# Halving the first gated-FFN weight unit, re-timing the weight and activation transfers, and adding the last outputs in DRAM

## The chip, the cores and the metric

The kernel is one launch on all eight cores of one Trainium2 chip (trn2). Each core works on its own prompt sequence and on 16 of the 128 sample tokens, with the same weights and without talking to the other cores. The metric is the device time of the slowest core, in microseconds (us). Executions of a program on all eight cores have a second, slower state here: the cores of one die run at a lower granted TensorE clock, and the time is some per cent longer.

The trace tells five engines apart: PE (TensorE, matrix products; "PEld" are its weight loads), DVE (VectorE), ACT (ScalarE), POOL (GpSimd) and SP (SyncE). The last two issue most of the DMAs.

## The reference, cut to what matters

```python
def _layer(x, buf_a, buf_b, h0, p):
    x = x + 0.5 * _rmsnorm(_swiglu(_rmsnorm(x, p['g_ffn1_pre']), ...), p['g_ffn1_post'])
    m, nba, nbb, hl = _mixer(_rmsnorm(x, p['g_mix_pre']), buf_a, buf_b, h0, p)
    x = x + _rmsnorm(m, p['g_mix_post'])
    x = x + 0.5 * _rmsnorm(_swiglu(_rmsnorm(x, p['g_ffn2_pre']), ...), p['g_ffn2_post'])
    return x, nba, nbb, hl

def _swiglu(x, w_gate, w_up, w_down):
    return (jax.nn.silu(x @ w_gate) * (x @ w_up)) @ w_down
```

The model width is 1024 (eight chunks of 128), the FFN width 2816 (22 "hidden blocks" of 128). A sequence has 2048 tokens and 16 meta tokens in front. Two places matter for this change: the first product, whose weights are the `gate` and `up` columns of hidden block 0, and the last line, a residual `x` plus a normed FFN output, which is what is stored.

## The kernel before

A core's 2080 tokens are cut into five streams of 414 to 418 tokens, which share three sets of activation buffers. The weights don't fit on the core, so they stream through a ring of ten slots, one "unit" of up to 128 x 2048 bf16 values per slot. The streams go through the layer in four groups. Group 0 (streams 0 and 1) reads the weights in fp32, casts them in the DMA and writes the bf16 form back to a scratch tensor `wsc`; later groups read the scratch. Stream 2 joins group 0 for the first `JOIN` units, so that the first hidden blocks have three streams to feed.

All instruction orders are fixed when the program is built: a list scheduler in the kernel's Python walks a model of the engines and of the DMA queues and picks what each engine issues next, steered by priority tables (`LAGS`, `STARTS`, `ENDS`, `CLASSES`). On the chip each engine then runs its list in that order and waits by semaphores.

```python
SIZES = [418, 418, 416, 414, 414]
GROUPS = [[0, 1], [2], [3], [4]]
BUFSET = [0, 1, 2, 0, 1]          # streams 3 and 4 take over the buffers of 0 and 1
NW = 10                           # slots of the weight ring
JOIN = 8
WARM = (44, 12, 10, 10, 40, 50)   # filler matmuls that keep TensorE busy at the start
X2_AFTER = 1
CAST_BW = 265e3; COPY_BW = 400e3  # bytes per us, the scheduler's model of the DMA

def issue_unit(g, u):
    n, off = UNIT_LIST[u][2], UNIT_OFF[u]
    v = V(wpool, lambda sl: wring[:, sl, :])                 # one slot of the ring
    src = wall if g == 0 else wsc
    S.dma("pool", lambda e: e.dma_start(out=v[0:n](), in_=src[:, off:off + n]), ..., cast=(g == 0))
    if g == 0:                                               # write the bf16 form back
        S.dma("sp", lambda e: e.dma_start(out=wsc[:, off:off + n], in_=v[0:n]()), [v], [("wsc", u)], n * 128 * 2)
    return v

def final_norm(st, acc):
    s, n, o, m = st.s, st.n, st.o, st.m
    rv = rms_finish(acc, m)
    step = 2 if st.last else 4
    events = []
    for oc in range(KC):
        yv = O32[s][:, oc * m:(oc + 1) * m]
        tv = newf()
        tt(tv[0:m], y32[s][:, oc, 0:m], rv[0:m], ALU.mult, m, ...)        # normed FFN output
        tt(yv, xs_view(st, oc, o, n), tv[0:m], ALU.add, m, ...)           # plus the residual
        if (oc + 1) % step == 0:
            ...                                                           # y store, issued by SP

def gu(st, hc, w, o):             # one hidden block of one stream
    ...
    ns = 8 if st.i == 0 and o == 0 and hc < 2 else 4 if hc < 2 else 1
    pG, pU, sg = newp(), newp(), newf()
    mm_split(pG[0:m], m, [wv(w, k * 128, 128) for k in range(KC)], rhs, rd, w, pG, ns)
    early = st.i == 0 and o == 0 and hc == 0
    mm_split(pU[0:m], m, [wv(w, (KC + k) * 128, 128) for k in range(KC)], rhs, rd, w, pU, ns, ...)
    if early:
        keep_warm(WARM[5], ["early"])       # 50 filler matmuls after stream 0's first block
    ...

# order of the first loads
first(-999.0, load_x, STREAMS[0], "sp", [])
head = [first(-998.0, issue_unit, 0, 0)]
first(-997.0, load_x, STREAMS[1], "pool", [R_xs(STREAMS[0], 3)])
head += [first(-997.0 + u, issue_unit, 0, u) for u in range(1, HEAD)]
```

## Time and profile before

The time was 1573.11 us (median of three runs, 1571.3 to 1598.96; the longest is in the slow state). From the first page of the profile of the slowest core: the span, the busy time of each engine with its share and its number of instructions, and the shares of the chain of waits that ended last.

```profile
span 1573.1 us, 27150 instructions; the slowest of 8 cores (1564.6 to 1573.1 us)
...
PE 1534.5 (98%) x8771; PEld 846.8 (54%) x8771; DVE 812.2 (52%) x1535; ACT 787.3 (50%) x1379; POOL 245.3 (16%) x465
...
PE 89%; DMA 5%; DVE 3%; issue 1%; ACT 1%; POOL 0%; DVEq 0%; SPq 0%; ACTq 0%; POOLq 0%
```

TensorE is the bound. Its 8,560 useful matmuls start 176 ns apart in the steady stretches (175.6 in the mean), which makes 1,503 us, so only about 70 us can be won by any change that leaves the matmuls alone. Most of them lie in four places.

| Where | What the trace shows | Lost there |
|---|---|---|
| head | few useful matmuls before 27.2 us | about 24 us (27.2 us less 16 x 0.176) |
| about 870 us | one gap, then half clock on six of the eight cores | 4 to 10 us, by core (time from the 4700th to the 4800th useful matmul, less 17.6) |
| tail | from the last matmul's start to the end | 14.5 us |
| small gaps elsewhere | | about 11 us |

The head, in the timeline view of TensorE (core 2). The columns are start, length, engine, source line, operation with its tiles, number of matmuls, and in brackets the idle time before and what ended it. "hy,wring" is useful work (activations with a weight slot), "qp,ones" are sums of squares for a norm, "ones" alone are fillers.

```profile
16.45 3.96 PE L652 MATMUL P<-hy,wring 128*128 128x418 bf16 x12 [2.06 <-DVE hy L684]
...
21.96 2.95 PE L652 MATMUL P<-ones 128*128 128x128 bf16 x50
...
27.21 54.13 PE L652 MATMUL P<-hy,wring 128*128 128x418 bf16 x304 [1.13 <-DMA wring<-wall]
82.16 0.34 PE L652 MATMUL P<-qp,ones 128*128 128x416 bf16 x1 [0.81 <-DVE qp L670]
```

The first hidden block of stream 0 starts at 16.45 us. Its last four matmuls stand between sums of squares of stream 1, which wait for that stream's input, fillers follow, and the second block starts at 27.21 us, when a weight unit from `wall` has landed. From there TensorE runs 54 us without a break, until stream 2 joins at 82 us with almost no wait.

The stall in the middle: TensorE's timeline on the same core, then that of SP, which issues the input of stream 3 (`xs<-xin`) and the outputs of stream 0 (`yout<-big`), 830 KB each.

```profile
867.15 2.97 PE L652 MATMUL P<-hy,wring 128*128 128x416 bf16 x16 [0.20 <-DMA wring<-wsc]
876.16 7.80 PE L652 MATMUL P<-hy,wring 128*128 128x416 bf16 x32 [6.04 <-DMA wring<-wsc]
```

```profile
854.30 0.33 SPq L740 DMA_DIRECT2D xs<-xin  x1
854.73 0.38 SPq L810 DMA_DIRECT2D yout<-big  x1
858.98 0.33 SPq L740 DMA_DIRECT2D xs<-xin  x1
859.40 0.41 SPq L810 DMA_DIRECT2D yout<-big  x1
```

TensorE stands for 6.04 us until a weight unit from the scratch lands. The 32 matmuls after that take 7.80 us where 5.6 would do: in the records of the clock it is at half there. The Trainium skill, "TensorE: Matmul & The Clock Gate", Part 1, says of the gate that answers to idleness that it knows only full and half, that the clock falls to half after about 3.4 us of idleness and needs about as long to come back. The half-clock stretches here are 3 to 10 us long. They show no fixed border in the length of a gap: in the run after, all eight cores have a gap of 2.21 or 2.22 us near 1230 us, shorter than the page's 3.4 us, and two of them show half clock behind it; in the run before, core 3 has none behind a gap of 3.89 us at 872 us. So a gap can cost more than its own length, but by how much differs from core to core.

The tail: VectorE's timeline (core 2), and from the view of DMAs in the last 20 us the line of the four y stores of the last stream (issuing queue, number, KB each, median us from issue to landing).

```profile
1560.30 0.59 DVE L670 TENSOR_TENSOR fp<-hy,fp 128x414 f32<-128x414 f32 x1 [4.09 <-ACT fp L666]
1561.00 0.59 DVE L670 TENSOR_TENSOR big<-xs,fp 128x414 f32<-128x414 f32 x1
...
1569.37 0.59 DVE L670 TENSOR_TENSOR big<-xs,fp 128x414 f32<-128x414 f32 x1
```

```profile
yout<-big SPq DMA_DIRECT2D x4, 414.0 KB, 2.4
```

The last matmul starts at 1558.6 us. After the norm's scale is known, VectorE makes 16 passes of 0.59 us, a product and a sum for each of the eight chunks, and each pair of chunks is stored when it is ready. VectorE sets the pace; only the last store is exposed.

### The profile page before, as it was taken

The page shows a single profiled execution, that of the slowest core. Times are in us where ns is not written, and L with a number is a line of the kernel's source. Part 1 is how long each engine was busy: PE and PEld are TensorE (multiplying, and loading weights), DVE is VectorE, ACT ScalarE, POOL GpSimd, SP SyncE. Part 2 cuts the span into 40 slices and gives each one's busy share as a digit, 9 for nine tenths or more (in the row PEclk, how much of TensorE's full clock was granted, in tenths as well). Part 3 has the DMA queues.
Part 4 walks back from the last instruction along what each step waited for, and adds up shares of the span by engine and source line. Part 5 has one row for each costly group of instructions (what it writes and reads, how often), then busy time and mean ns, then how long its engine had stood idle before and what let it go on. Part 6 is the DMA issues. An engine that isn't in the chain of part 4 may idle for free.

```text
span 1573.1 us, 27150 instructions; the slowest of 8 cores (1564.6 to 1573.1 us)
## 1 busy us (share of the span) xinstructions
PE 1534.5 (98%) x8771; PEld 846.8 (54%) x8771; DVE 812.2 (52%) x1535; ACT 787.3 (50%) x1379; POOL 245.3 (16%) x465
## 2 busy tenths in 40 slices
PE   8999999999999999999999899999999999999996
PEld 5555555555555555555555455555555555555553
DVE  3232128987786465832136451374667886752143
ACT  4221137888766576521154421446765788352232
POOL 1001111011101111111111122221221111112220
PEclk9999999999999999999999999999999999999998
DMA  8979869568785875998967685655586545565662
GB/s 195 233 150 196 177 161 205 164 156 217 163 186 156 219 191 171 199 190 181 203 168 192 213 262 177 215 172 181 173 249 208 177 158 187 174 198 172 191 209 86
DMA packets 80393, 293.82 MB, mean 187 GB/s; under 512 B 9600, under 2 KB 9728, under 8 KB 80256
## 3 DMA queue, kind: packets, MB, share of 16 engines
q0 software_dynamic: 60240, 222.07, 59.5%
q1 hardware_dynamic: 20016, 70.02, 11.7%
q8 instruction: 74, 1.21, 0.3%
q14 instruction: 63, 0.52, 0.1%
HBM read 283.71 MB, written 64.45 MB: 221 GB/s over the span
## 4 chain that ended last, share of the span: by engine, by line
PE 89%; DMA 5%; DVE 3%; issue 1%; ACT 1%; POOL 0%; DVEq 0%; SPq 0%; ACTq 0%; POOLq 0%
PE P L652 89%; DMA wring<-wsc 3%; DMA wring<-wall 2%; DVE fp L684 1%; DVE fp L670 1%; DVE big L670 1%; ACT fp L666 0%; DMA xs<-xin 0%; DVE fp L689 0%; DVE xs L694 0%; ACT L666 0%; DVEq L1088 0%; DVE fp L678 0%; DVE hy L684 0%; POOL xs L740 0%
## 5 line engine op out<-in xcount | busy, mean ns | idle before, releaser
L652 PE MATMUL P<-hy,wring 128*128 128x414 bf16 (+4 forms) x6080 | 1099.7, 339 | 17.5 <-DMA wring<-wsc 10.2
L652 PEld LDWEIGHTS P<-hy,wring 128*128 128x128 bf16 x6080 | 589.5, 97 | 501.3 <-issue 29.4
L666 ACT ACTIVATE fp<-P 128x414 f32<-128x414 f32 (+4 forms) x529 | 267.6, 516 | 603.4 <-PE P L652 589.4
L652 PE MATMUL P<-big,wring 128*128 128x414 bf16 (+3 forms) x2400 | 444.1, 339 | 1.0 <-ACT fp L666 0.7
L670 DVE TENSOR_TENSOR big<-P,fp 128x414 bf16<-128x414 f32 (+3 forms) x260 | 151.0, 588 | 384.1 <-PE P L652 364.1
L652 PEld LDWEIGHTS P<-big,wring 128*128 128x128 bf16 x2400 | 233.7, 97 | 190.6 <-issue 3.2
L720 POOL DMA_DIRECT2D wring<-wsc x340 | 180.9, 532 | 814.1 <-PE P L652 791.0
L670 DVE TENSOR_TENSOR fp<-fp 128x414 f32<-128x414 f32 (+4 forms) x215 | 122.8, 572 | 153.4 <-ACT fp L666 146.7
L666 ACT ACT_TABLE_LOAD x96 | 123.2, 1283 | 43.5 <-PE P L652 34.9
L720 POOL DMA_DIRECT2D wring<-wall x116 | 61.5, 534 | 467.0 <-PE P L652 379.6
L666 ACT ACTIVATE fp<-fp 128x414 f32<-128x414 f32 (+2 forms) x230 | 121.2, 545 | 15.4 <-DVE fp L684 5.7
L684 DVE SCALAR_TENSOR_TENSOR fp<-P,par_sb,fp 128x418 f32<-128x418 f32 (+3 forms) x120 | 77.5, 646 | 20.8 <-ACT fp L666 13.0
L684 DVE SCALAR_TENSOR_TENSOR hy<-xs,par_sb,fp 128x414 bf16<-128x414 f32 (+3 forms) x120 | 69.0, 646 | 27.0 <-ACT fp L666 26.9
L666 ACT ACTIVATE fp<-xs 128x414 f32<-128x414 f32 (+3 forms) x104 | 54.6, 544 | 27.3 <-DVE xs L670 18.9
L684 DVE SCALAR_TENSOR_TENSOR fp<-fp,P 128x414 f32<-128x414 f32 (+3 forms) x80 | 45.2, 581 | 38.8 <-PE P L652 34.0
L670 DVE TENSOR_TENSOR fp<-hy,fp 128x414 f32<-128x414 f32 (+3 forms) x80 | 46.8, 585 | 17.7 <-ACT fp L666 17.6
L684 DVE SCALAR_TENSOR_TENSOR fp<-fp,par_sb 128x402 f32<-128x402 f32 (+4 forms) x80 | 51.5, 644 | 7.6 <-DVE fp L678 0.5
L666 ACT ACTIVATE fp<-fp,dpar 128x418 f32<-128x418 f32 (+2 forms) x80 | 51.1, 639 | 5.6
L666 ACT ACTIVATE hy<-P,dpar 128x414 f32<-128x414 f32 (+3 forms) x80 | 48.5, 607 | 7.1
L666 ACT ACTIVATE fp<-P,dpar 128x418 f32<-128x418 f32 (+2 forms) x80 | 44.2, 605 | 11.2 <-PE P L652 6.7
L670 DVE TENSOR_TENSOR xs<-xs,fp 128x414 f32<-128x414 f32 (+3 forms) x80 | 47.0, 588 | 5.0 <-DVE fp L670 0.3
L689 DVE TENSOR_TENSOR_SCAN fp<-fp,CAR 128x418 f32<-128x418 f32 (+3 forms) x40 | 43.1, 1077 | 4.1 <-DVE fp L670 0.5
(44 smaller groups left out, 378.5 us busy)
## 6 DMA issues: line engine op xcount, KB each, us to landing
wring<-wsc POOLq DMA_DIRECT2D x244, 512.0 KB, 4.8
wring<-wall POOLq DMA_DIRECT2D x84, 512.0 KB, 9.0
wsc<-wring SPq DMA_DIRECT2D x84, 512.0 KB, 8.8
wring<-wsc POOLq DMA_DIRECT2D x96, 352.0 KB, 3.9
wring<-wall POOLq DMA_DIRECT2D x32, 352.0 KB, 7.7
wsc<-wring SPq DMA_DIRECT2D x32, 352.0 KB, 5.5
xs<-xin SPq DMA_DIRECT2D x4, 828.0 KB, 11.2
xs<-xin SPq DMA_DIRECT2D x4, 418.0 KB, 6.8
```

Source lines behind the costliest of these rows:

```text
L652: ins = e.matmul(o, ev(lhs_list[k]), ev(rhs_list[k]), start=(start and k == 0), stop=(stop and k == nk - 1))
L666: return S.op("act", lambda e: e.activation(out=ev(out), in_=ev(in_), func=func, **kw), reads, writes, dur, tbl=TBL.get(func), prio=prio)
L670: return S.op("dve", lambda e: e.tensor_tensor(out=ev(out), in0=ev(in0), in1=ev(in1), op=op), reads, writes, 0.153 + n / 960.0, prio=prio)
L684: return S.op("dve", lambda e: e.scalar_tensor_tensor(out=ev(out), in0=ev(in0), scalar=scalar, in1=ev(in1), op0=op0, op1=op1), reads, writ ...
L689: return S.op("dve", lambda e: e.tensor_tensor_scan(out=ev(out), data0=ev(d0), data1=ev(d1), initial=init, op0=ALU.mult, op1=ALU.add), rea ...
L720: S.dma("pool", lambda e: e.dma_start(out=v[0:n](), in_=src[:, off:off + n]), [R_xs(STREAMS[0], 3)] if g == 0 else [("wsc", u)], [v, ("wl" ...
```

## The change

Its intent has four parts.

1. **Head.** The gate and the up columns of hidden block 0 become two units of half the size (the code calls them `GQ`), so that the first matmuls need only 0.5 MB of fp32 weights instead of 1 MB. The write-backs of the first units wait until four units have landed. `JOIN` goes from 8 to 7 units; as two of those are halves, this is six hidden blocks shared by three streams, where it was eight.
2. **Middle.** The outputs of streams 0 and 1 are stored only when the next input of the same buffer has landed, so that the two transfers no longer interleave.
3. **Tail.** The residual of the last stream is written to its place in the output early, under matmuls. At the end VectorE only multiplies (eight passes), and GpSimd issues DMAs that add the product to what lies in DRAM.
4. **Re-timing.** All priority tables are new, the model takes 320 KB/us for inputs, and allows 1.0 us more before a matmul that waits for a DMA.

The diff, cut to its core (the number tables, which are most of its length, are left out):

```diff
-JOIN = 8
+JOIN = 7
+ACC_TAIL = True
+ACC_BW = 200e3
@@ the list of units
-    for i in range(HC):
+    u.append(("GQ", 0, 1024, 8))
+    u.append(("GQ", 1, 1024, 8))
+    for i in range(1, HC):
         u.append(("GU1", i, 2048, 16))
@@ the scheduler's model
-DMA_CAP = (0.75, 0.95)
+INPUT_BW = 320e3
+DMA_CAP = (0.72, 0.95)
+PE_MARGIN_DMA = 1.0
@@ issue_unit: write-backs
-                S.dma("sp", lambda e: e.dma_start(out=wsc[:, off:off + n], in_=v[0:n]()),
-                      [v], [("wsc", u)], n * 128 * 2)
+                backs.append((v, u, n, off))
+                for v_, u_, n_, off_ in list(backs) if u >= HEAD - 1 else ():
+                    S.dma("sp", ..., [v_] + ([("wl", 0, HEAD - 1)] if u_ < HEAD else []), [("wsc", u_)], n_ * 128 * 2)
+                    backs.pop(0)
@@ final_norm
-                tv = newf()
-                tt(tv[0:m], y32[s][:, oc, 0:m], rv[0:m], ALU.mult, m, R_y32(oc, s) + [rv], [tv])
-                tt(yv, xs_view(st, oc, o, n), tv[0:m], ALU.add, m, [R_xs(st, oc), tv], [("o32", s, oc)])
+                tv = None if st.last and ACC_TAIL else newf()
+                tt(yv if tv is None else tv[0:m], y32[s][:, oc, 0:m], rv[0:m], ALU.mult, m, ...)
+                if tv is not None:
+                    tt(yv, xs_view(st, oc, o, n), tv[0:m], ALU.add, m, [R_xs(st, oc), tv], [("o32", s, oc)])
+                if st.last and (oc + 1) % 2 == 0:
+                    events.append((add_y if ACC_TAIL else store_y)(st, oc - 1, oc + 1))
+        def keep_x(st):                      # called long before, after the second norm's residual
+            S.dma("sp", lambda e: e.dma_start(out=dst, in_=XS[st.s][:, 0:KC * m]), ..., ["yx"], KC * m * 512)
+        def add_y(st, k0, k1):
+            return S.dma("pool", lambda e: e.dma_start(out=dst, in_=src, accum_op=ALU.add),
+                         [("o32", s, k) for k in range(k0, k1)] + ["yx"], [], (k1 - k0) * m * 512, bw=ACC_BW)
@@ y stores of the other streams
+                    follower = [x for x in STREAMS if x.i > i and x.s == st.s]
+                    for k0 in (0, 4) if not st.last else ():
+                        stores.append((follower, g, u, st, k0))
...
+                    for fo, g0, u0, st, k0 in [x for x in stores if x[0][0].i == i]:
+                        out_events.append(at(g0, u0, "post", st, store_y, st, k0, k0 + 4,
+                                             [R_xs(STREAMS[i], k) for k in range(KC)]))
```

## The prediction

> **What bounds the kernel now.** TensorE: 98% of the 1573.1 us span by the page, 89% of the chain of waits. Matmuls start 176 ns apart (median in the trace), so 8,560 useful ones need 1,503 us; only the other 70 us can be won.
> - Head, 27 us (timeline). The first 1 MB weight unit lands at about 16.3 us; stream 0's activations appear from 14.5 us, 0.58 us a chunk; stream 1's 1.67 MB load next; the second unit lands at 27.2 us. Until then 16 useful matmuls ran. Unit 0's write-back shares the DMA engines from 20 to 26 us.
> - A stall at 869.8 us: a start-to-start gap of 6.4 us (3.5 to 7.5 us over the eight cores), released by a weight load from scratch, then 7 us at half clock in the clock record (3 to 10): 5 to 12 us together. SP interleaves x loads and y stores of 830 KB there.
> - Tail, 14.5 us from the last matmul: norm scale, 16 VectorE passes of 0.59 us (1560.3 to 1570.0 us), and the last 414 KB store, 2.4 us to land.
> - Small gaps elsewhere, 11 us in all.
>
> **What the change does, costed.**
> 1. Head: gate and up of the first hidden block become half-size units, stream 1 still loads between them, write-backs wait for four units to land. By the packet record's bytes, the gate half lands near 13.5 us (the activations then set the start, 14.6 us), the up half near 20.5, the next full unit near 24 instead of 27.2. Gain 3 us. The join falls from 8 to 7 units (6 hidden blocks shared by three streams, before 8); that leaves one hidden block less (5.6 us of PE) to cover stream 2's load, which should come earlier. No net loss.
> 2. Middle: y stores of streams 0 and 1 wait until the next x of that buffer has landed. The 869 us stall should mostly go: 8 us. Other re-timing: 2 us, either sign.
> 3. Tail: 8 of 16 VectorE passes go, 4.7 us, but the addition becomes four 414 KB accumulating DMAs. The Trainium skill, "DMA: Bandwidth & Descriptors", Rules for kernel authors, has these issued from GpSimd (0.53 us an issue here); "Collectives: The Full Stack", Part 3, says such an add reads two sources per write. This trace has none. Plain pieces moved at about 400 GB/s; at half of that (an estimate from the page) four need 8 us from the first ready piece (1561.5 us), so the queue ends the program. Net gain 1 to 2 us. The early residual write lies under matmuls: free.
>
> **Sum.** 3 + 8 + 2 + 1.5, about 14 us, on the critical path because PE is. Discounted for new stalls: 1560 us, 8 in 10 between 1550 and 1570. Faster by over 2%: 0.03; within 2%: 0.95; slower: 0.02.
>
> **What would show each step.** PE timeline: the second hidden block starts by 24 to 25 us; no gap over 2 us at 860 to 875 us, no half clock there; last matmul about 12 us earlier. SP: x loads before y stores. Tail: VectorE ends 6.5 us after the last matmul, not 11.5; accumulate DMAs take over 4 us to land; tail 12 to 13.5 us.
>
> **What would make it wrong.** Accumulating far slower than half rate (tail over 18 us); a new stall where stream 2 joins (65 to 85 us) or near 1250 us; the x load, not the y stores, starving the weights at 869 us.

## The result

The changed kernel took 1569.87 us (median of four runs, 1566.71 to 1875.57; the longest is a slow-state run in which one die had a clock of 0.81 to 0.82), against 1572.2 us (median of four, one of them slow) before. The ratio is 0.9981, with a 95% interval of 0.9961 to 1.0001. A ratio here is the mean time of one kernel's fast runs over that of the other's fast runs of the same rounds, so it isn't quite the ratio of the medians. A second measurement (experiment e11) gave 0.9974 (0.9961 to 0.9987). So the change gains 2 to 4 us, where 13 had been predicted. "Within 2%" was right and the time lies just inside the predicted range, but the predicted gain was three to six times too large.

From the first page of the profile after:

```profile
span 1568.8 us, 27188 instructions; the slowest of 8 cores (1561.8 to 1568.8 us)
...
PE 1532.2 (98%) x8771; PEld 846.6 (54%) x8771; DVE 808.4 (52%) x1527; ACT 772.1 (49%) x1367; POOL 251.2 (16%) x474
...
PE 92%; DMA 3%; DVE 2%; issue 1%; ACT 1%; POOL 0%; DVEq 0%; POOLq 0%; SPq 0%; ACTq 0%
```

The matmuls are the same and the page looks the same: totals don't say where 13 us went. A better tool is a race: count the useful matmuls on each core, and ask at which time each kernel starts the next one. The table gives means of all eight cores, worked out from the two traces; a positive difference is a gain. "Last" is the last useful matmul. The tail below it starts at the last matmul of all, a sum for the last norm, which starts 1.1 us later.

| After so many useful matmuls | before, us | after, us | gained so far | stage |
|---|---|---|---|---|
| 0 | 16.4 | 15.2 | +1.2 | first matmul |
| 8 | 17.9 | 22.6 | -4.7 | gate done, up begins |
| 16 | 27.0 | 27.4 | -0.4 | second hidden block |
| 200 | 60.3 | 60.0 | +0.2 | |
| 300 | 78.0 | 82.2 | -4.2 | stream 2 joins |
| 400 | 97.2 | 100.0 | -2.8 | |
| 4700 | 859.3 | 860.5 | -1.2 | ahead of the stall |
| 4800 | 884.1 | 879.6 | +4.5 | behind it |
| last | 1553.1 | 1546.7 | +6.4 | |

| Stretch | before, us | after, us |
|---|---|---|
| tail: last matmul's start to the end, mean of eight cores | 14.5 | 17.4 (16.4 to 18.4) |

Summed up: the head and the join lose 2.8 us where +3 and 0 were predicted; the rest up to the last matmul gains 9.2 us where 10 was predicted; the tail loses 2.9 us where +1.5 was predicted. These are single profiled executions, good to 2 or 3 us: in the repeat e11 the head and the join lost 1.4 us, the rest gained 10.4, so that the last useful matmul started 9.0 us earlier than before (mean of eight cores), not 6.4, and its tails were 16.3 to 18.0 us. The sum of this table, 3.5 us, agrees with the ratios.

**Head and join after** (TensorE's timeline, core 1):

```profile
15.56 0.34 PE L660 MATMUL P<-hy,wring 128*128 128x418 bf16 x1 [0.90 <-DVE hy L692]
17.07 0.34 PE L660 MATMUL P<-qp,ones 128*128 128x418 bf16 x1 [1.17 <-ACT qp L674]
...
20.88 0.95 PE L660 MATMUL P<-qp,ones 128*128 128x418 bf16 x2 [1.03 <-ACT qp L674]
...
25.26 2.95 PE L660 MATMUL P<-ones 128*128 128x128 bf16 x50
28.05 48.34 PE L660 MATMUL P<-hy,wring 128*128 128x418 bf16 x272
79.22 0.48 PE L660 MATMUL P<-qp,ones 128*128 128x416 bf16 x1 [2.83 <-DVE qp L678]
```

The first matmul is earlier. But between the gate matmuls the fixed order has put sums of squares of stream 1, which wait for stream 1's input, and the 50 fillers still stand behind the block. The second block starts at 28.05 us, and nothing is named as its releaser: it waited for no load. Its weight unit had landed at 24.4 us on this core by the semaphore that tells of the landing (22.7 to 25.8 us over the eight cores), as predicted, and so 1.7 to 4.2 us before the block started. The load came earlier, but the matmuls did not.

At the other end, TensorE's unbroken stretch ends at 76.4 us instead of 82, and it then waits about 3 us for the norm of stream 2. All eight cores show this gap, and seven of them half clock for 3.4 us after it (in the repeat e11 only one). Stream 2's input had landed long before. The first fence is from the view of the input tile, same core, window 20 to 80 us: its ScalarE passes (shortest, median and longest in ns, first and last start in us), its two DMA issues, and their time to landing. The second is ScalarE's timeline.

```profile
L674 ACT ACTIVATE fp<-xs x8: 536/540/542, 65.7 to 76.9; 128x416 f32<-128x416 f32 x8
...
L754 POOL DMA_DIRECT2D xs<-xin x2: 535/541/547, 21.9 to 22.4; - x2
...
DMA to landing us min/median/max: 33.9/35.5/37.1
```

```profile
65.68 0.98 ACT L674 ACTIVATE fp<-xs 128x416 f32<-128x416 f32 x2
...
69.88 0.98 ACT L674 ACTIVATE fp<-xs 128x416 f32<-128x416 f32 x2
...
75.54 1.85 ACT L674 ACTIVATE fp<-xs 128x416 f32<-128x416 f32 x4
```

The input was issued at 21.9 and 22.4 us and landed 33.9 and 37.1 us later, so at about 56 and 59.5 us. Its eight squares run from 65.7 to 77.4 us, spread out, because the build's own model had the two halves landing at 62.9 and 69.4 us and placed the squares accordingly behind other work of ScalarE.

**The middle after** (TensorE, then SP, core 1):

```profile
868.77 5.79 PE L660 MATMUL P<-hy,wring 128*128 128x416 bf16 x32 [2.22 <-DMA wring<-wsc]
```

```profile
854.42 5.01 SPq L754 DMA_DIRECT2D xs<-xin  x2
869.14 0.82 SPq L844 DMA_DIRECT2D yout<-big  x2
```

The outputs now follow the inputs, the gap shrinks from 6.04 to 2.22 us, and 32 matmuls take 5.79 us instead of 7.80: no half clock. From the 4700th to the 4800th useful matmul the kernel gains 5.7 us (6.0 in e11), where 8 was predicted for the stall.

**The tail after** (core 1): VectorE and GpSimd in the timeline, then from the DMA view of 1550 to 1570 us what was moved in 40 slices of 0.5 us, and the time to landing.

```profile
1554.19 4.09 DVE L678 TENSOR_TENSOR big<-hy,fp 128x414 f32<-128x414 f32 x8 [5.01 <-ACT fp L674]
1555.92 3.74 POOL L837 DMA_DIRECT2D yout<-big  x4 [22.41 <-DVE big L678]
```

```profile
GB/s 0 0 0 0 0 0 0 0 0 0 0 0 0 0 79 26 0 7 152 199 212 199 179 212 212 199 212 205 212 212 212 212 205 205 40 0 0 0 0 0
...
yout<-big POOLq DMA_DIRECT2D x4, 414.0 KB, 7.5
```

VectorE is done at 1558.28 us, 5.8 us after the last matmul, as predicted. But the four adding DMAs then run at about 210 GB/s until 1567.3 us. They take 7.5 us to land (median), where the stores of the kernel before took 2.4; part of this is waiting behind one another, but the first, with none ahead of it, took 4.9 to 7.0 us by core. The queue ends the program.

### The profile page after: what moved, and what is told of

Its sections match the earlier page's. It is cut to its first block, busy times and chain, and to the rows that moved or that the text cites. A ratio compares the mean times of both kernels' runs of the same rounds, so it can differ in the third digit from the quotient of the medians.

```text
span 1568.8 us, 27188 instructions; the slowest of 8 cores (1561.8 to 1568.8 us)
## 1 busy us (share of the span) xinstructions
PE 1532.2 (98%) x8771; PEld 846.6 (54%) x8771; DVE 808.4 (52%) x1527; ACT 772.1 (49%) x1367; POOL 251.2 (16%) x474
## 3 DMA queue, kind: packets, MB, share of 16 engines
q1 hardware_dynamic: 19728, 70.02, 12.1%
## 4 chain that ended last, share of the span: by engine, by line
PE 92%; DMA 3%; DVE 2%; issue 1%; ACT 1%; POOL 0%; DVEq 0%; POOLq 0%; SPq 0%; ACTq 0%
PE P L660 92%; DMA wring<-wsc 2%; DMA xs<-xin 1%; DVE fp L692 1%; ACT fp L674 0%; DVE fp L678 0%; DVE big L678 0%; ACT L674 0%; DVE xs L702 0%; DVE fp L697 0%; DVE fp L686 0%; DVE qp L678 0%; DVEq L1137 0%; ACT qp L674 0%; DVE xs L678 0%
## 5 line engine op out<-in xcount | busy, mean ns | idle before, releaser
L678 DVE TENSOR_TENSOR fp<-fp 128x414 f32<-128x414 f32 (+3 forms) x215 | 122.5, 572 | 131.2 <-ACT fp L674 124.3
L674 ACT ACTIVATE fp<-fp 128x418 f32<-128x418 f32 (+2 forms) x230 | 121.1, 545 | 13.3 <-DVE fp L692 4.0
L692 DVE SCALAR_TENSOR_TENSOR fp<-P,par_sb,fp 128x418 f32<-128x418 f32 (+3 forms) x120 | 77.4, 646 | 25.0 <-ACT fp L674 16.9
L678 DVE TENSOR_TENSOR fp<-hy,fp 128x418 f32<-128x418 f32 (+3 forms) x72 | 42.1, 584 | 10.6 <-ACT fp L674 10.6
```

The lines of the kernel that those rows point to most:

```text
L674: return S.op("act", lambda e: e.activation(out=ev(out), in_=ev(in_), func=func, **kw), reads, writes, dur, tbl=TBL.get(func), prio=prio)
L678: return S.op("dve", lambda e: e.tensor_tensor(out=ev(out), in0=ev(in0), in1=ev(in1), op=op), reads, writes, 0.153 + n / 960.0, prio=prio)
L692: return S.op("dve", lambda e: e.scalar_tensor_tensor(out=ev(out), in0=ev(in0), scalar=scalar, in1=ev(in1), op0=op0, op1=op1), reads, writ ...
```

## The experiments

Twelve kernels ran in three jobs. The median of the kernel before was 1573.51, 1575.89 and 1573.44 us in them, so compare ratios rather than microseconds across jobs. The run after is from an earlier measurement. In the table, the last matmul is the last useful one.

| Run | this, us (median) | ratio to before (95%) | last useful matmul, us (mean of cores) | tail, us |
|---|---|---|---|---|
| after | 1569.87 | 0.9981 (0.9961 to 1.0001) | 1546.7 | 16.4 to 18.4 |
| e11 after, again | 1569.61 | 0.9974 (0.9961 to 0.9987) | 1544.1 | 16.3 to 18.0 |
| e1 plain tail | 1567.62 | 0.9955 (0.9941 to 0.9969) | 1545.6 | 14.2 to 14.5 |
| e2 adding tail alone | 1577.6 | 1.0025 (1.0013 to 1.0038) | 1552.5 | 19.3 to 20.6 |
| e3 fewer fillers | 1568.81 | 0.9971 (0.9955 to 0.9986) | 1545.9 | 16.4 to 17.9 |
| e4 halves in one slot | 1568.72 | 0.9966 (0.9953 to 0.998) | 1546.1 | 16.6 to 18.3 |
| e5 earlier norm of stream 2 | 1567.02 | 0.9944 (0.9929 to 0.9958) | 1543.2 | 17.4 to 18.6 |
| e6 outputs not held back | 1582.78 | 1.0045 (1.0032 to 1.0058) | 1559.5 | 16.7 to 17.7 |
| e7 first unit whole again | 1568.37 | 0.9955 (0.9943 to 0.9967) | 1545.8 | 17.1 to 18.6 |
| e8 e1 + e3 + e4 + e5 | 1561.34 | 0.9914 (0.9901 to 0.9926) | 1542.0 | 14.2 to 14.4 |
| e9 e8, stream 1's input later | 1560.68 | 0.9919 (0.9906 to 0.9933) | 1540.5 | 14.2 to 14.4 |
| e10 e8, half of the tail adding | 1560.64 | 0.9923 (0.9911 to 0.9936) | 1541.2 | 13.6 to 14.8 |
| e12 the four DMAs without the addition (output wrong) | 1602.54 (two of four runs slow) | 0.9923 (0.9905 to 0.9942) | 1544.4 | 10.9 to 11.5 |

The theory: the tail and the join each lose about what the head was to gain, and the middle is the only part that pays. The rivals, one for each part, are named with the experiments.

### The tail: e1, e2, e12, e10

**e1** takes the adding tail out of the changed kernel; otherwise the instruction order of every engine is the same.

```diff
-ACC_TAIL = True
+ACC_TAIL = False
```

> The changed kernel with its tail undone: the last stream is finished by 16 VectorE passes and plain stores from SP, as before; the instruction order of every other part is the same. In the changed kernel the last matmul starts at 1546.7 us (mean of the eight cores) and the tail is 16.4 to 18.4 us, mean 17.4; in the kernel before the tail is 14.5 us. Theory (the accumulating DMAs cost more than the 8 VectorE passes save): tail 14.5 us again on every core, last matmul unmoved near 1546.7, total about 3 us below the changed kernel, near 1566 to 1567 us. Rival (the tail is longer because all cores reach it closer together[...], or because GpSimd starts late for another reason): the tail stays above 16 us.

Measured: 1567.62 us, ratio 0.9955. The last useful matmul starts at 1545.6 us, 1.1 us earlier than in the run after and 1.5 later than in e11, which is within the spread of single profiles, and the tail is back at 14.2 to 14.5 us on all cores. The line of the last stores in the DMA view of 1548 to 1562 us (core 6):

```profile
yout<-big SPq DMA_DIRECT2D x4, 414.0 KB, 2.7
```

So the adding tail costs the change 2 to 4 us, by medians and by ratios; the traces put it at 3 us.

**e2** is the converse: only the adding tail and the early residual write, put into the kernel before.

```diff
-                tt(tv[0:m], y32[s][:, oc, 0:m], rv[0:m], ALU.mult, m, R_y32(oc, s) + [rv], [tv])
-                tt(yv, xs_view(st, oc, o, n), tv[0:m], ALU.add, m, [R_xs(st, oc), tv], [("o32", s, oc)])
+                tt(yv if tv is None else tv[0:m], y32[s][:, oc, 0:m], rv[0:m], ALU.mult, m, ...)
+                if tv is not None:
+                    tt(yv, xs_view(st, oc, o, n), tv[0:m], ALU.add, m, ...)
+                if st.last and (oc + 1) % step == 0:
+                    events.append(add_y(st, oc - 1, oc + 1))
...
+                        at(g, u, "pre", st, keep_x, st)
```

> The kernel before with only the accumulating tail and the early residual write added; everything else in the same order. Theory: the last matmul stays at 1553.1 us in the mean of the cores (the 1.65 MB residual write is hidden), the tail grows from 14.5 to 16.4 to 18.4 us, total 2 to 4 us slower than the kernel before, about 1575 us. Rival (the accumulating tail as such gains, as the prediction said, and the loss comes from its combination with the other parts): tail 12 to 13.5 us, total about 1571 us.

Measured: slower than before, 1.0025 (1.0013 to 1.0038), about 4 us. The tail was 19.3 to 20.6 us, more than expected. The last matmul did not move (1552.5 against 1553.1 us), so the early residual write is free, as predicted. The extra 2 to 3 us of tail are not explained: the last packets were done 15.0 to 16.7 us after the last matmul, but GpSimd's closing instruction ended 3.4 us after the last landing, where in the run after it ended 0.8 us after it (on every core). In direction, e2 confirms e1.

**e12** asks what it is in the adding DMA that costs: the same four DMAs from the same engine, without the addition. Its outputs are wrong on purpose (the last stream lacks its residual).

```diff
-            return S.dma("pool", lambda e: e.dma_start(out=dst, in_=src, accum_op=ALU.add),
+            return S.dma("pool", lambda e: e.dma_start(out=dst, in_=src),
```

> The changed kernel with the accumulation taken off its last four DMAs, which are otherwise the same (issued from GpSimd, same pieces). The result is wrong on purpose for the last stream's rows: the residual is overwritten. It tells the cost of adding from the cost of issuing on GpSimd. Theory (the add in flight is what is slow[...]): each piece takes about 1.3 us as in the plain tail instead of 2.3 to 4 us, the pieces follow the issues at 4.9 to about 9 us, tail 10.5 to 11.5 us. Rival (the path from GpSimd and its end of work set the tail): pieces stay above 2 us or the tail above 14 us.

The rate in slices of 0.35 us and the time to landing, from the DMA view of 1548 to 1562 us (core 2):

```profile
GB/s 0 0 0 0 0 0 0 0 0 0 0 0 0 0 435 435 341 265 341 322 284 379 435 322 360 379 454 95 0 0 0 0 0 0 0 0 0 0 0 0
...
yout<-big POOLq DMA_DIRECT2D x4, 414.0 KB, 3.2
```

The tail fell to 10.9 us (11.5 on one core). So the halved VectorE work is worth 3.6 us, well over the 1.5 predicted for the step as a whole, but the addition in flight takes back 6.5 us (17.4 less 10.9). It costs in two ways: half the rate, and 0.84 to 0.90 us of GpSimd for an issue instead of 0.54. The adding DMAs also move their 1.70 MB in 576 packets, where e12 has 320; but the plain stores of the kernel before have 576 too and land in 2.4 us, so the number of packets alone is not the cost. The Trainium skill, "DMA: Bandwidth & Descriptors", Anatomy of one DMA, fits such a DMA with 2.0 us and 436 GB/s; that makes 3.0 us for 414 KB (an estimate from the page), and e12's 3.2 us agree. With the addition the trace has 7.5 us. Only two of e12's four runs were fast, so its ratio, 0.9923, is left out of the argument; the trace carries it.

**e10** was to save the idea: add only the first four chunks in DRAM, while VectorE makes both passes for the last four, which are stored plainly by SP. It is built on e8 below.

```diff
+ACC_CHUNKS = 4
...
-                tv = None if st.last and ACC_TAIL else newf()
+                added = st.last and oc < ACC_CHUNKS
+                tv = None if added else newf()
...
-                    events.append((add_y if ACC_TAIL else store_y)(st, oc - 1, oc + 1))
+                    events.append((add_y if added else store_y)(st, oc - 1, oc + 1))
```

> The combined candidate with a mixed tail: the first four of eight chunks of the last stream are added by two accumulating DMAs, the last four by VectorE with plain stores. From the measured tails: VectorE ends at 9.0 instead of 11.4 us after the last matmul, the last plain piece lands at about 11.7 us, the two accumulating pieces end at about 10.3 us and need 1.5 to 2 us more. Theory: tail 12 to 12.6 us instead of 14.3, total about 2 us below the combined candidate. Rival (GpSimd's end of work, which came 0.5 to 3.5 us after the last landing in the accumulating tails, rules): tail 13 to 15 us, no gain.

Measured: 1560.64 us, the same as e8 (1561.34) within the intervals, and tails of 13.6 to 14.8 us. VectorE was done 8.6 us after the last matmul instead of 11.4. But the first packet of the first plain piece, issued at 6.3 us, came 1.7 to 3.4 us after the issue (0.8 us in e1), and the second piece ended at 12.5 to 13.5 us: they shared the DMA engines with the adding pieces, whose last packets ran until 10.6 to 12.4 us. The Trainium skill, "DMA: Bandwidth & Descriptors", Issuing engines are not separate DMA queues, says that DMAs of all engines share the same 16 DMA engines and interleave. The trace agrees with both: on every core 32 to 113 packets of the adding pieces began after the first packet of the plain ones.

### The head and the join: e3, e4, e5, e7, e9

**e3** cuts the fillers behind stream 0's first block from 50 to 4.

```diff
-WARM = (44, 12, 10, 10, 40, 50)
+WARM = (44, 12, 10, 10, 40, 4)
```

> The changed kernel with the 50 filler matmuls behind the first up group cut to 4. In the changed kernel the second unit's packets end at 22.4 to 24.9 us, yet its first matmul comes at 27.6 us (mean), just after 2.95 us of filler. Theory (the head gain was there but the filler and then the join of stream 2 ate it): the second hidden block starts 2 to 3 us earlier, near 25 us; the two first streams then run out of work 2 to 3 us earlier before stream 2 joins near 76 us, so the gap there grows from 3 to about 5 to 6 us and the total stays within 1 us of the changed kernel. Rival A (the filler is the whole loss): last matmul and total 2.5 us earlier. Rival B (the weight, not the filler, set the start): the second block still starts at 27 us.

TensorE's timeline (core 3):

```profile
24.13 0.38 PE L660 MATMUL P<-ones 128*128 128x128 bf16 x4
25.67 48.35 PE L660 MATMUL P<-hy,wring 128*128 128x418 bf16 x272 [1.15 <-DVE hy L692]
77.78 0.50 PE L660 MATMUL P<-qp,ones 128*128 128x416 bf16 x1 [3.75 <-DVE qp L678]
```

(By the semaphore, the landing of the second unit is at 22.7 to 25.8 us, as said above.) The work after the first 16 matmuls began 2.1 us earlier (25.3 us, mean of the cores), but the gap at the join grew from 2.83 to 3.75 us, on every core. After 400 useful matmuls 1.1 us were left, and nothing against e1, which has the head and the join of the run after and ran in the same job. The total, 0.9971, can't be told from that of the run after. Here a head start is worth nothing while a later wait has a fixed end: TensorE merely arrives earlier at the wait for stream 2.

**e4** tests why TensorE runs dry at 76 us instead of 82. Each half unit takes a whole slot of the ring of ten, so nine hidden blocks instead of ten can be held before stream 2 joins, and a block of two streams is 5.6 us of matmuls. Here both halves share one slot.

```diff
-            v = V(wpool, lambda sl: wring[:, sl, :])
+            second = g == 0 and u == 1
+            v = V(wpool, lambda sl: wring[:, sl, :]) if not second else qslot[0]
...
+                i = S.dma("pool", lambda e: e.dma_start(out=v[1024:1024 + n](), in_=src[:, off:off + n]), ...)
```

> The changed kernel with the two half-size first units in the two halves of one weight slot during the first pass, so that ten hidden blocks instead of nine fit in the ring of ten slots before stream 2 must join. Theory (a half unit occupies a whole slot, so the change took 5.6 us of TensorE work away from the wait for stream 2): the 3.2 us gap near 76 us disappears, with the half-clock record after it, and the progress at the 300th to 800th matmul is 2.5 to 4.5 us earlier than in the changed kernel; total about 3 us less. Rival (stream 2's activations are late for another reason, its norm being placed late in ScalarE's fixed order): the gap only moves to about 82 us and the gain is under 1 us.

Measured: the gap at 76 us is gone, and after 300 matmuls the kernel is 4.5 us earlier than the one after. But gaps of 0.7 us near 82 us and 1.3 us near 87 us appear on every core, 1.7 us are left after 400 matmuls, and the total is 0.9966 (0.9953 to 0.998). That lies between theory and rival: the slot is one reason for the gap, but stream 2's norm moved back along with it in the fixed order.

**e5** goes for that order. In the schedule's model stream 2's input gets 480 KB/us instead of 320, so that the squares are placed earlier. No transfer is different in itself.

```diff
-                      [R_xs(st, k) for k in range(k0, k0 + step)], step * st.n * 512, bw=INPUT_BW)
+                      [R_xs(st, k) for k in range(k0, k0 + step)], step * st.n * 512, bw=480e3 if st.i == 2 else INPUT_BW)
```

> The changed kernel with one number of the ordering changed: the order is made as if stream 2's input moved at 480 instead of 320 KB per us, so the squares of its norm stand earlier in ScalarE's fixed order; transfers and work are the same. In the changed kernel stream 2's packets end at 58 to 63 us, but its last squares run at 75.5 to 77.4 us and TensorE waits 3.2 us for the sum at 79 us, then loses up to 3.5 us more at half clock. Theory (the order was made for a landing at 69 us and holds the norm back): the norm is done by about 72 us, the 3.2 us gap and the half-clock record near 80 us vanish, and progress at the 400th matmul and the last matmul are 2.5 to 4 us earlier; total about 3 us below the changed kernel. Rival (the ring's nine hidden blocks are the limit): the gap stays over 2 us, gain under 1 us.

ScalarE's last square of stream 2, then TensorE at the join (core 7):

```profile
73.00 0.54 ACT L674 ACTIVATE fp<-xs 128x416 f32<-128x416 f32 x1
```

```profile
54.79 21.95 PE L660 MATMUL P<-hy,wring 128*128 128x418 bf16 x123
76.58 0.34 PE L660 MATMUL P<-qp,ones 128*128 128x416 bf16 x1
76.76 18.55 PE L660 MATMUL P<-hy,wring 128*128 128x418 bf16 x104
```

The squares end at 73.5 us instead of 77.4, and TensorE passes the join without a gap and without half clock. After 400 matmuls the kernel is 3.7 us earlier than the one after, at the last useful matmul 3.5 us (against e11, 2.2 and 0.9 us). No core has a gap over 0.6 us between 60 and 100 us. The ratio is 0.9944 (0.9929 to 0.9958); the median is 2.9 us lower than that of the run after. So the wait at the join was made by the placing of the norm, not by the transfer. (e4, and e7 below, close most of the gap the other way, with one more block to work on, but have lost most of the lead by the 400th matmul.)

**e7** makes the first unit whole again and leaves the rest of the change.

```diff
-    u.append(("GQ", 0, 1024, 8))
-    u.append(("GQ", 1, 1024, 8))
-    for i in range(1, HC):
+    for i in range(HC):
         u.append(("GU1", i, 2048, 16))
...
+    LAGS = LAGS[:1] + LAGS[2:]      # and the same for the other tables; JOIN 6, HEAD 3, X2_AFTER 0, RG_AFTER 11
```

> The changed kernel with its first weight unit whole again (gate and up of the first hidden block in one slot), the table entry of the second half dropped, six blocks shared by three streams as in the changed kernel; deferred write-backs, y order and accumulating tail stay. Theory (the halves gain nothing, because the second block still waits for the same bytes, and cost a ring slot): the second hidden block starts within 1 us of the changed kernel's 27.6 us, the 3.2 us gap near 76 us goes or shrinks below 1.5 us, and the total is 1.5 to 3 us below the changed kernel. Rival (the halves gain the 3 us of the prediction and something else loses it): the second block starts 2 to 3 us later than in the changed kernel, total 2 to 3 us above.

Measured: the second hidden block starts at 27.3 us, with the halves it was 27.4. The halves, the part that gives the change its name, gain nothing there, though they bring the landing of the next unit forward by about 1 us (24.5 against 25.6, means). After 48 useful matmuls the kernel with the whole unit is 1.3 us behind the run after and 0.5 us behind e5 of the same job. With the ring slot back the gap at the join is down to one of 0.8 us and one of 1.3 us, on every core. The ratio, 0.9955 (0.9943 to 0.9967), is a little lower than with the halves, but its interval overlaps both of theirs.

**e9** (on e8) loads stream 1's input behind the second block's weights, to ask whether the head is limited by the order of the loads.

```diff
-        first(-997.0, load_x, STREAMS[1], "pool", [R_xs(STREAMS[0], 3)])
+        first(-994.5, load_x, STREAMS[1], "pool", [R_xs(STREAMS[0], 3)])
```

> The combined candidate with one more change at the head: stream 1's input (1.67 MB) is loaded behind the second hidden block's weights instead of ahead of the first block's up half, so stream 0 has two blocks to do while stream 1 loads. Theory (the head is paced by bytes that land, not by TensorE): stream 0's second block starts at 20 to 22 us instead of 27.0, stream 1's first at 27 to 29 us, and progress at the 48th matmul improves by 1 to 3 us; total 1 to 2.5 us below the combined candidate, if the join near 80 us does not wait. Rival (it only shifts which stream waits): 48th matmul within 0.7 us, same total.

TensorE's timeline (core 0):

```profile
20.82 3.70 PE L660 MATMUL P<-hy,wring 128*128 128x418 bf16 x20 [0.21 <-DMA wring<-wall]
...
31.40 42.68 PE L660 MATMUL P<-hy,wring 128*128 128x418 bf16 x240 [0.28 <-DVE hy L692]
```

Sixteen useful matmuls are done 6.5 us earlier than in e8, at 20.4 us. But after 48 the lead is 0.4 us: now TensorE waits for stream 1. The ratio, 0.9919, is that of e8. So the rival held: the order of the loads only shifts which stream waits. That the bytes needed by about 32 us are the limit fits this, but only this one other order was tried.

### The middle: e6

**e6** lets the outputs of streams 0 and 1 go as soon as they are ready, as before, in the changed kernel.

```diff
-                    follower = [x for x in STREAMS if x.i > i and x.s == st.s]
+                    follower = []
```

> The changed kernel with the y stores of streams 0 and 1 issued as before, as soon as each half is ready and between the x loads of the streams that follow; weights and other orders are made by the same tables. Theory (the order of x loads and y stores removed the stall near 869 us): the stall comes back, a gap of 3.5 to 7.5 us near 865 to 870 us with a half-clock record after it, and the saving over the kernel before between the 4700th and 4800th matmul (5.7 us in the changed kernel) falls to under 2 us; total about 4 to 5 us above the changed kernel. Rival (the re-timed weights removed it): gaps there stay under 3 us and the total is within 1.5 us.

TensorE's timeline (core 3):

```profile
865.67 4.51 PE L660 MATMUL P<-hy,wring 128*128 128x416 bf16 x16 [3.18 <-DMA wring<-wsc]
872.80 7.47 PE L660 MATMUL P<-hy,wring 128*128 128x416 bf16 x32 [2.62 <-DMA wring<-wsc]
...
932.62 12.56 PE L660 MATMUL P<-hy,wring 128*128 128x414 bf16 x54 [4.43 <-DMA wring<-wsc]
```

The stall is back, in two parts, and a second one appears at 925 to 933 us, each with half clock after it. The last matmul is 12.8 us later than in the run after, and the kernel is slower than before, 1.0045 (1.0032 to 1.0058). So in the new order it is holding back the outputs that removed the stall, as predicted, and not the re-timing alone; whether it would be enough in the old order, no run shows. Without it the re-timed order loses more than the old one did, so 10 to 13 us (by ratios and by traces) is what this part is worth inside the new order, and the 5.7 us gained between matmuls 4700 and 4800 is what the whole change gained over the old kernel there. The order of TensorE, ScalarE and VectorE also shifts a little behind 863 us in e6, as the list is made anew.

### A version that beats both: e8

**e8** joins what the parts taught: plain tail (e1), four fillers (e3), both halves in one slot (e4), the earlier norm (e5).

```diff
-ACC_TAIL = True
+ACC_TAIL = False
-WARM = (44, 12, 10, 10, 40, 50)
+WARM = (44, 12, 10, 10, 40, 4)
...
+                      ..., bw=480e3 if st.i == 2 else INPUT_BW)
```

> A candidate: the changed kernel with the plain tail, the two first half units in one slot, the filler cut from 50 to 4, and the early norm of stream 2. If the losses that the single runs show add up: tail 14.3 us, second hidden block at 25.3 us, no gap over 1.5 us near 80 us; last matmul at about 1541 us in the mean and a total of 1560 to 1562 us, ratio to the kernel before about 0.992. If they are not independent (what is gained before stream 2 joins is waited for at the next fixed point): 1564 to 1566 us.

TensorE's timeline (core 0):

```profile
15.92 0.34 PE L660 MATMUL P<-hy,wring 128*128 128x418 bf16 x1 [1.32 <-DVE hy L692]
21.17 0.51 PE L660 MATMUL P<-qp,ones 128*128 128x418 bf16 x1 [4.91 <-ACT qp L674]
...
28.62 54.02 PE L660 MATMUL P<-hy,wring 128*128 128x418 bf16 x304 [1.16 <-DVE hy L692]
82.48 0.34 PE L660 MATMUL P<-qp,ones 128*128 128x416 bf16 x1
```

Measured: 1561.34 us, 0.9914 (0.9901 to 0.9926), so 13.5 us faster than before and 8 to 10 us faster than the change as given. No gap over 1.5 us is left near 80 us, and the tails are 14.2 to 14.4 us. One expectation failed: the first 16 useful matmuls were not over by 25.3 but by 26.9 us (mean), because TensorE stood 4.91 us between the first and the second gate matmul, waiting for the squares of stream 1.

### The repeat: e11

> The changed kernel itself again, unedited, on the chip of these runs and in the same rounds, so that the differences to it are paired: ratio 0.997 to 1.000 to the kernel before, last matmul 1546 to 1548 us, tail 16.4 to 18.5 us, a 3.2 us gap near 76 us on every core.

**e11** is the changed kernel again, unedited, beside the others of the third job: 1569.61 us, 0.9974 (0.9961 to 0.9987). The gap at the join was there on every core (2.83 us idle, 3.2 us from start to start). The gain of 2 to 4 us is real, and small.

## Why the prediction was right or wrong

The prediction's size was wrong: 13 us were forecast and 2 to 4 measured. Three of its steps failed, the head, the join and the tail; the join and the tail took back more than half of what the middle had gained.

1. **Bound and total.** Right: TensorE is still busy 98% of the span, and all that moved lies in the gaps named beforehand.
2. **"Gain 3 us" at the head: wrong.** The bytes behaved as predicted (the next unit had landed by 22.7 to 25.8 us, 24 was said). The step that failed is the last one, from "the next full unit lands near 24" to "the second hidden block starts by 24 to 25 us". It started at 27.4 us (27.0 before), behind sums of squares of stream 1 and 2.95 us of fillers that the fixed order puts there. e3 shows that taking the fillers away brings that start forward by 2.1 us, e7 that the half units do not bring it forward at all.
3. **"No net loss" at the join: wrong.** After 300 useful matmuls 4.2 us were lost (2.8 in e11). The prediction saw the hidden block less, 5.6 us of work, and set against it that stream 2's input comes earlier. It did come about 10 us earlier. But the norm that turns it into work stood where the schedule's model had put it. e5 moves that norm, and the gap is gone: 3.7 us are won at the 400th matmul (2.2 against e11). The new stall "where stream 2 joins (65 to 85 us)" was listed under what would make the prediction wrong, but nothing was subtracted for it in the sum beyond a general discount.
4. **Middle, 8 + 2 us: right in mechanism and in sum, the split partly luck.** 9.2 us were gained behind the join, but 5.7 at the stall, where 8 was said, and 3.5 elsewhere, where 2 of either sign was said. e6 shows that the held-back outputs removed the stall; what made the other 3.5 us, no run shows.
5. **"Net gain 1 to 2 us" in the tail: wrong in sign.** VectorE ended as predicted and the half rate was about right (199 to 212 GB/s in the trace of core 1; the median packet took 272 ns on every core, 131 in the plain stores before, both of 3,312 bytes). The mis-sized term is "four need 8 us from the first ready piece": from the ready piece to the first packet 2.1 us passed, 0.9 of them the issue, and from the first packet to the last 10.1 to 12.1 us by core (10.0 to 11.4 in e11), as the first piece began slowly and some packets took far longer than the median. To this come 1.4 us to the end. The tail was 17.4 us, not 12 to 13.5. e1 and e2 agree on the direction, and by e12 the addition in flight costs 6.5 us, while the shorter VectorE work saves 3.6.

Left open: why e2's closing instruction on GpSimd came 2.5 us later behind the last landing than that of the run after, and how much the re-timed tables give by themselves; no run has only them.

## What to carry to other kernels

At the very end of this program the adding DMA is itself the critical path, and it ran at half the rate of a plain store and cost more than the passes it replaced; whether it would pay under other work, no run here shows. An earlier load paid here only where what consumes it was also placed earlier: in a kernel with a fixed instruction order, look for the instruction that stands between the landing and the use, and for the next wait that has a fixed end. Hold output stores back while the next inputs and weights compete for the same DMA engines; that was the one part of this change that paid.

## What the Trainium skill lacked or had wrong

- "DMA: Bandwidth & Descriptors" says that a DMA that adds is issued from GpSimd, and this kernel does so, but gives no cost. Here, 414 KB pieces into DRAM took 7.5 us to land (median of four; the first, with none ahead of it, 4.9 to 7.0 by core) where plain ones took 3.2 us from the same engine (e12) and 2.4 us from SP (before); an issue took 0.84 to 0.90 us instead of 0.54.
- "Collectives: The Full Stack", Part 3, gives half the rate for a reduction with two reads, for collectives. For a kernel's own adding DMA this fits as a rate, 199 to 212 GB/s in the trace of core 1 against about 400 for plain stores, and the median packet took 272 ns against 131. No page says that single packets take longer still: the means by core were 306 to 367 ns in the run after and 311 to 353 in e11.
- "DMA: Bandwidth & Descriptors" says that DMAs of different issuers interleave. They do in e10, but the page doesn't say what that costs a store behind adding DMAs: the first packet of SP's plain piece came 1.7 to 3.4 us after its issue, where it came after 0.8 us in e1.
- No page tells what GpSimd's closing instruction waits for; it ended 0.8 us after the last landing in the run after, and 3.4 us after it in e2.
